# Two up products made while the last two tiles' gates are built, and two instead of three one-hot buffers in that gate building

## The chip, the cores and the metric

The kernel runs on one core of a Trainium2 chip. The metric is device time in microseconds (us), the median of the runs shown. The engines are named as in the profile: PE (TensorE matmuls, with PEld for its weight loads), DVE (VectorE), ACT (ScalarE), POOL (GpSimd, which issues the gathers) and SP (SyncE, which issues the other DMAs).

## The reference

The layer mixes 1024 tokens of width 1024 and then applies a PEER block: each token picks, for each of 8 heads, its 16 best of 16384 one-neuron experts and sums their outputs under a softmax gate.

```python
top, pos = lax.top_k(cand, PEER_TOPK)
idx = jnp.take_along_axis(cidx, pos, axis=-1)
gates = jax.nn.softmax(top, axis=-1)
u_sel = expert_u[idx]
act = gelu(einsum('thkd,td->thk', u_sel, xb))
v_sel = expert_v[idx]
return einsum('thk,thkd->td', gates * act, v_sel)
```

## The kernel before

The 8 tiles of 128 tokens are treated in two ways. Three tiles (0, 6, 7) are "sparse": the rows of u and v are gathered by POOL, and DVE forms the dot products (L547) and the weighted sums (L556). Five tiles (1 to 5; 640 tokens) are "dense": all 16384 experts are computed on PE in 128 blocks ("chunks") of 128 experts, and a dense gate matrix G, zero where an expert is not chosen, scales the activations.

The stages that matter here follow each other so:

- **Gate stage A** (`gates` with `who` "A", 48 blocks of 8 tokens for the first three dense tiles) is interleaved with the queries of the second half. **Gate stage B** (`who` "AT", 32 blocks for the last two dense tiles) comes after it, alone. A block makes two one-hot arrays and multiplies them on PE (L595), which gives the gates of 8 tokens. `o2` (L576, DVE, float32) is the first one-hot; `o1` (L582 or L588, DVE) the second; `og` is `o1` times the gate, made by ACT in 8 instructions (L585, an "A" block) or by DVE in one (L590, a "T" block). ACT moves the product from PSUM into `stg` (L597), and every fourth block SP stores `stg` to `G_dr` in HBM (L599). In the trace each 128x128 float32 matmul of L595 is recorded as two instructions. The buffer counts are three for `o2`, two for `og`, three for `o1`, four banks for the PSUM tile `pt`.
- **Dense stage**: `up(c)` loads the chunk's G (every fourth chunk, L639), u and v, splits u and v into a high and a low part (L183 on ACT, L184 on DVE), makes the up product on PE (24 matmuls for each half of the 640 tokens, tile `pu`), applies Gelu (L652, ACT), multiplies by G (L653, DVE) and splits the result (L656 on ACT, L657 on DVE). `down` multiplies the results of three chunks by v (tiles `pv` and `pa`), and DVE adds `pv` to the accumulators (L670).

In the kernel before, u of chunk 0 is loaded and split ahead of gate stage B (the name `u0`), and everything else of `up` lies behind it. When gate stage B ends, its SBUF pool and the PSUM pool are closed and the dense stage's pools take their place, so that tiles of the dense stage can lie where `stg` lay.

What order the instructions have on each engine is decided by the framework's planner: of the instructions that are ready by its own costs, it takes the one that was written first in the program. Each engine then runs its list in that order and stops at an instruction whose wait is not over. The sparse tiles' DVE work is written last and fills in; `pace` ties each piece from number 70 on to a chunk's first G product (`marks`). All loads and stores other than gathers are issued by SP, in order.

Of the kernel before, what the change touches and what calls it, by code (L numbers as in the profile page):

```python
# [45 lines left out]
GV = 3  # L46
AB = 2
GB = 3
RB = 4
VB = 7  # L50
DORD = [2, 0, 3, 1, 4]
# [20 lines left out]
def block_kernel(ctx: ExitStack, tc: tile.TileContext, x, attn_g, w_in, conv_w, sgu_wT, sgu_b, sgu_g,  # L72
# [119 lines left out]
    def mm3(o, lh, ll, rh, rl, first, last):  # L192
        pe.matmul(o, lh, rh, start=first, stop=False)  # L193
        pe.matmul(o, lh, rl, start=False, stop=False)  # L194
        pe.matmul(o, ll, rh, start=False, stop=last)  # L195
# [371 lines left out]
    def gates(pool, tiles, n0, n1, who):  # L567
        nblk = 0
        for n in range(n0, n1):
            stg = pool.tile([P, NCH // CB, TB, CB], F32, name="stg", bufs=2)  # L570
            for b in range(TB // OB):
                tt = n * TB + b * OB
                d, db = DT[tiles[tt // P]]
                tl = tt % P
                o2 = pool.tile([P, OB, P], F32, name="o2", bufs=3)
                v_.tensor_tensor(o2, iota_k.unsqueeze(1).to_broadcast([P, OB, P]),  # L576
                                 d[:, 0, tl:tl + OB].unsqueeze(2).to_broadcast([P, OB, P]), ALU.is_equal)
                nblk += 1
                og = pool.tile([P, OB, P], F32, name="og", bufs=OGB)
                if who[nblk % len(who)] == "A":  # L580
                    o1 = pool.tile([P, P, OB], BF16, name="o1", bufs=O1B)
                    v_.tensor_tensor(o1, iota_r, db[:, tl:tl + OB].unsqueeze(1).to_broadcast([P, P, OB]),  # L582
                                     ALU.is_equal)
                    for m in range(OB):
                        a_.activation(og[:, m, :], o1[:, :, m], AF.Copy, scale=d[:, 1, tl + m:tl + m + 1])  # L585
                else:
                    o1 = pool.tile([P, OB, P], BF16, name="o1", bufs=O1B)
                    v_.tensor_tensor(o1, iota_b.unsqueeze(1).to_broadcast([P, OB, P]),  # L588
                                     db[:, tl:tl + OB].unsqueeze(2).to_broadcast([P, OB, P]), ALU.is_equal)
                    v_.tensor_tensor(og, o1, d[:, 1, tl:tl + OB].unsqueeze(2).to_broadcast([P, OB, P]), ALU.mult)  # L590
                for q in range(OB // 4):
                    o = ps.tile([P, 4, P], F32, name="pt", bufs=4)
                    for i in range(4):
                        m = q * 4 + i
                        pe.matmul(o[:, i, :], o2[:, m, :], og[:, m, :], start=True, stop=True)  # L595
                    dst = stg[:, :, b * OB + q * 4:b * OB + q * 4 + 4, :].rearrange("p c t m -> p t c m")
                    a_.activation(dst, o.rearrange("p t (c m) -> p t c m", m=CB), AF.Copy)  # L597
                if b == TB // OB - 1:
                    nc.sync.dma_start(G_dr[:, :, n * TB:(n + 1) * TB, :], stg)  # L599
                yield  # L600
# [8 lines left out]
    def load(up_, src):  # L609
        raw = up_.tile([P, KC, P], F32, name="raw", bufs=RB)  # L610
        nc.sync.dma_start(raw, src)
        return split(up_, raw, [P, KC, P], "u", 2)

    def dense(pool, up_, pacc, pps, tiles, hD, u0):
        hTh, hTl = hD
        nt = len(tiles)
        HALF = TD // 2
        accs, full = {}, {}
# [16 lines left out]
        def up(c):  # L635
            if c % CB == 0:
                for hf in range(2):
                    Gt[hf] = pool.tile([P, HALF, CB], F32, name="G", bufs=GB)
                    nc.sync.dma_start(Gt[hf], G_dr[:, c // CB, hf * HALF:(hf + 1) * HALF, :])  # L639
            uh, ul = load(up_, peer_uT[c]) if c else u0  # L640
            raw = up_.tile([P, KC, P], F32, name="raw", bufs=RB)
            nc.sync.dma_start(raw, peer_v[c * P:(c + 1) * P, :].rearrange("e (k d) -> e k d", d=P))
            v = [split(pool, raw[:, 4 * dh:4 * dh + 4, :], [P, 4, P], "v", VB) for dh in range(2)]
# [1 line left out]
            wl = pool.tile([P, TD], F32R, name="wl", bufs=GV + 1)  # L645
            for hf in range(2):
                sl = slice(hf * HALF, (hf + 1) * HALF)
                o = pps.tile([P, HALF], F32, name="pu", bufs=2)
                for k in range(KC):
                    mm3(o, uh[:, k, :], ul[:, k, :], hTh[:, k, sl], hTl[:, k, sl], k == 0, k == KC - 1)  # L650
                a = pool.tile([P, HALF], F32, name="a", bufs=AB)
                a_.activation(a, o, AF.Gelu)  # L652
                gm = v_.tensor_tensor(a, a, Gt[hf][:, :, c % CB], ALU.mult)  # L653
                if hf == 0:
                    marks.append(gm)
                a_.activation(wh[:, sl], a, AF.Copy)  # L656
                v_.tensor_tensor(wl[:, sl], a, wh[:, sl].bitcast(F32), ALU.subtract)  # L657
# [79 lines left out]
    rx = ExitStack()  # L737
    hD = load_hD(sb(rx, "hdp", side="right"))
    up_ = sb(rx, "uvp", side="right")
    u0 = load(up_, peer_uT[0])  # L740
    with ExitStack() as c1:
        gp = sb(c1, "gpB")
        take(gates(gp, D_TILES, nA, NTB, OGPB))
    dkx.close()
    pre.close()
    with ExitStack() as c2:
        pool = sb(c2, "dl")
        pacc = c2.enter_context(tc.tile_pool(name="pacc", bufs=1, space=PSUM))
        pps = c2.enter_context(tc.tile_pool(name="pps", bufs=2, space=PSUM))
        dense(pool, up_, pacc, pps, D_TILES, hD, u0)  # L750
        sparse(spool, S_TILES)
    rx.close()

# [39 lines left out]
```

## Time and profile before

| What | Value |
|---|---|
| Median of 3 runs | 2833.63 us (2823.56 to 2846.36) |
| The profiled execution's own time | 2831.65 us |
| Its span | 2829.9 us, 40392 instructions |
| Busy share of the span: PE, DVE, ACT, POOL | 94%, 86%, 39%, 43% |
| Mean DMA rate | 251 GB/s |

The shares are means over stages with different limits. The stage before the gates ends near 628 us, gate stage A runs from about 628 to 902 us, gate stage B from about 905 to 998 us, and the dense stage fills the rest. PE's busy time is modelled from pipelined matmuls, so what a matmul costs is better read from the starts of a run of them.

### The profile page before, as it was taken

Reading aid. Unit: us, or ns where it says so; the run is one execution under the profiler, and the core shown is the slowest. Engines: PE = TensorE matmul, PEld = TensorE weight load, DVE = VectorE, ACT = ScalarE, POOL = GpSimd, SP = SyncE. Lnnn points to the kernel's source line nnn. Section 1 sums busy time; section 2 is a strip of 40 time slices with the busy share of each in tenths; the row PEclk is TensorE's granted clock in tenths of the full one; section 3 lists DMA queues with packets and bytes.
Section 4 is the critical chain, followed back from the end, with each engine's and each line's share of the span. In section 5 each row is a group of like instructions: output and inputs, shape, how many; then the busy total and the mean of one; then the engine's idle time right before and its main releaser. Section 6 shows DMA issues by size and latency. Waiting matters only on the chain.

```text
span 2829.9 us, 40392 instructions
## 1 busy us (share of the span) xinstructions
PE 2654.0 (94%) x14243; PEld 2325.6 (82%) x14243; DVE 2426.4 (86%) x4973; ACT 1102.9 (39%) x2125; POOL 1215.8 (43%) x1224
## 2 busy tenths in 40 slices
PE   8998889968885879999999999999999999999998
PEld 6876777756774768899888899899989889888987
DVE  3347978888989979999999999998998899898894
ACT  5324343249996932232333232323232222222223
POOL 0000013242002058777776666665555555455540
PEclk9999988888997999999999999999999999999999
DMA  3225225485447698988888897898888888888882
GB/s 123 82 81 191 81 69 172 137 304 150 141 125 264 197 348 313 332 297 318 324 301 323 314 325 292 310 333 314 306 323 316 303 318 305 296 325 282 305 320 75
DMA packets 270364, 709.96 MB, mean 251 GB/s; under 512 B 21576, under 2 KB 112720, under 8 KB 269904
## 3 DMA queue, kind: packets, MB, share of 16 engines
q0 software_dynamic: 110592, 402.70, 39.7%
q1 hardware_dynamic: 159568, 304.67, 31.2%
q8 instruction: 112, 1.84, 0.3%
q14 instruction: 92, 0.75, 0.1%
HBM read 650.14 MB, written 57.15 MB: 250 GB/s over the span
## 4 chain that ended last, share of the span: by engine, by line
PE 41%; DVE 16%; issue 7%; ACT 6%; DMA 5%; POOL 1%; SPq 0%; DVEq 0%; ACTq 0%; POOLq 0%
PE pu L193 6%; PE pu L194 6%; PE pu L195 6%; ACT og L585 4%; PE pv L193 4%; PE pv L195 4%; PE pv L194 4%; DVE gx L547 3%; DMA gx<-peer_u,si 3%; DVE acc L556 3%; PE pa L193 3%; PE pa L194 3%; PE pa L195 3%; PE pt L595 2%; DVE a L653 2%
## 5 line engine op out<-in xcount | busy, mean ns | idle before, releaser
L540 POOL DMA_INDIRECT gx<-peer_u,si x384 | 514.7, 1340 | 558.7 <-DVE dots L547 354.5
L540 POOL DMA_INDIRECT gx<-peer_v,si x384 | 538.3, 1402 | 350.8 <-DVE acc L556 239.1
L193 PE MATMUL pu<-hD,uh 128*128 128x320 f32 x2048 | 634.2, 310 | 17.3 <-ACT a L652 16.5
L195 PE MATMUL pu<-hD,ul 128*128 128x320 f32 x2048 | 633.5, 309 | 0.0
L194 PE MATMUL pu<-hD,uh 128*128 128x320 f32 x2048 | 633.3, 309 | 0.0
L556 DVE SCALAR_TENSOR_TENSOR acc<-gx,dots,acc 128x1024 f32<-128x1024 f32 x384 | 491.2, 1279 | 11.7 <-DMA gx<-peer_v,si 7.4
L547 DVE CUSTOM_DVE_ANT_0 gx<-gx,hn 128x1024 f32<-128x1024 f32 x384 | 460.1, 1217 | 16.3 <-DMA gx<-peer_u,si 13.5
L193 PEld LDWEIGHTS pu<-hD,uh 128*128 128x128 f32 x2048 | 384.9, 188 | 20.8 <-ACT a L652 18.3
L194 PEld LDWEIGHTS pu<-hD,uh 128*128 128x128 f32 x2048 | 385.2, 188 | 1.8
L195 PEld LDWEIGHTS pu<-hD,ul 128*128 128x128 f32 x2048 | 384.9, 188 | 0.0
L183 ACT ACTIVATE vh<-raw 128x512 fp32r<-128x512 f32 x256 | 160.9, 633 | 511.6 <-PE pv L195 487.8
L193 PE MATMUL pv<-vh,wh 128*128 128x512 f32 x768 | 302.2, 393 | 19.9 <-DVE ac L670 19.3
L656 ACT ACTIVATE wh<-a 128x320 fp32r<-128x320 f32 x256 | 120.9, 472 | 492.6 <-DVE a L653 479.4
L195 PE MATMUL pv<-vh,wl 128*128 128x512 f32 x768 | 301.1, 392 | 0.0
L194 PE MATMUL pv<-vl,wh 128*128 128x512 f32 x768 | 300.3, 391 | 0.0
L423 POOL TENSOR_TENSOR cidx<-i,i 128x8 f32<-128x8 f32 (+5 forms) x280 | 100.0, 386 | 361.3 <-DVE sel L450 163.1
L653 DVE TENSOR_TENSOR a<-a,G 128x320 f32<-128x320 f32 x256 | 186.6, 729 | 67.8 <-ACT a L652 67.8
L193 PE MATMUL pp<-Xh,wh 128*128 128x512 f32 x576 | 240.2, 418 | 3.1 <-ACT wh L183 3.1
L195 PE MATMUL pp<-Xh,wl 128*128 128x512 f32 x576 | 238.8, 415 | 3.3 <-DVE wl L184 3.3
L194 PE MATMUL pp<-Xl,wh 128*128 128x512 f32 x576 | 239.3, 416 | 0.0
L595 PE MATMUL pt<-og,o 128*128 128x128 f32 x1280 | 207.4, 306 | 30.1 <-ACT og L585 25.4
L585 ACT ACTIVATE og<-o,dT 128x128 f32<-128x128 bf16 x512 | 226.3, 518 | 5.8 <-DVE o L582 5.8
(188 smaller groups left out, 4670.9 us busy)
## 6 DMA issues: line engine op xcount, KB each, us to landing
raw<-peer_uT SPq DMA_DIRECT2D x128, 512.0 KB
raw<-peer_v SPq DMA_DIRECT2D x128, 512.0 KB
G_dr<-stg SPq DMA_DIRECT2D x20, 2048.0 KB
G<-G_dr SPq DMA_DIRECT2D x64, 640.0 KB
wraw<-w_in SPq DMA_DIRECT2D x40, 512.0 KB
wraw<-w_q SPq DMA_DIRECT2D x32, 512.0 KB
xt<-x SPq DMA_DIRECT2D x16, 512.0 KB
wraw<-w_out SPq DMA_DIRECT2D x16, 512.0 KB
```

The costliest lines, as they stand in the source:

```text
L183: a_.activation(hi, raw, AF.Copy)
L193: pe.matmul(o, lh, rh, start=first, stop=False)
L194: pe.matmul(o, lh, rl, start=False, stop=False)
L195: pe.matmul(o, ll, rh, start=False, stop=last)
L423: i = eng.tensor_tensor(dst[:, :, c:c + n], second[:, :, b0:b0 + n], first[:, :, a0:a1].to_broadcast([P, nt, n]), ALU.add)
L540: gp_.indirect_dma_start(out=gx, out_offset=None, in_=tab, in_offset=bass.IndirectOffsetOnAxis(ap=ii[:, s:s + 1], axis=0))
L547: pace(v_.tensor_tensor_reduce(gu, gu, hn, 1.0, 0.0, ALU.mult, ALU.add, dots[:, s:s + 1]), slot[0])
L556: pace(v_.scalar_tensor_tensor(acc, gv, dots[:, s:s + 1], acc, op0=ALU.mult, op1=ALU.add), slot[0])
L585: a_.activation(og[:, m, :], o1[:, :, m], AF.Copy, scale=d[:, 1, tl + m:tl + m + 1])
L595: pe.matmul(o[:, i, :], o2[:, m, :], og[:, m, :], start=True, stop=True)
L653: gm = v_.tensor_tensor(a, a, Gt[hf][:, :, c % CB], ALU.mult)
L656: a_.activation(wh[:, sl], a, AF.Copy)
```

## The change

A function `product` now makes an up product (24 matmuls and the Gelu for one half). For chunks 0 and 1 it is called from the gate stage B part: u of the chunk is loaded and split, both halves are multiplied into PSUM tiles of the tag `pp` (four banks that the queries used before and that the gate stage leaves alone), and the Gelu writes to two new SBUF tiles (`a0`, `a1`, 128x640 float32 each). Chunk 0 is written ahead of the first 16 blocks of stage B, chunk 1 ahead of the second 16. In the dense stage `up(0)` and `up(1)` then skip load, split, product and Gelu of u, and take the ready activations. The buffer count of `o2` is 2 in `gates`, which both gate stages call.

```diff
-                o2 = pool.tile([P, OB, P], F32, name="o2", bufs=3)
+                o2 = pool.tile([P, OB, P], F32, name="o2", bufs=2)
...
+    def product(pspool, tag, bufs, uh, ul, hD, sl, a):
+        o = pspool.tile([P, TD // 2], F32, name=tag, bufs=bufs)
+        for k in range(KC):
+            mm3(o, uh[:, k, :], ul[:, k, :], hD[0][:, k, sl], hD[1][:, k, sl], k == 0, k == KC - 1)
+        a_.activation(a, o, AF.Gelu)
...
-            uh, ul = load(up_, peer_uT[c]) if c else u0
+            pre_a = early.get(c)
+            if pre_a is None:
+                uh, ul = load(up_, peer_uT[c])
...
+                if pre_a is None:
+                    a = pool.tile([P, HALF], F32, name="a", bufs=AB)
+                    product(pps, "pu", 2, uh, ul, hD, sl, a)
+                else:
+                    a = pre_a[:, sl]
...
-    u0 = load(up_, peer_uT[0])
+    pf = sb(rx, "pf", side="right")
+    early = {}
     with ExitStack() as c1:
-        gp = sb(c1, "gpB")
-        take(gates(gp, D_TILES, nA, NTB, OGPB))
+        gg = gates(sb(c1, "gpB"), D_TILES, nA, NTB, OGPB)
+        nblk = (NTB - nA) * (TB // OB)
+        for c in range(PF):
+            early[c] = pf.tile([P, TD], F32, name=f"a{c}")
+            uh, ul = load(up_, peer_uT[c])
+            for hf in range(2):
+                sl = slice(hf * TD // 2, (hf + 1) * TD // 2)
+                product(ps, "pp", 4, uh, ul, hD, sl, early[c][:, sl])
+            take(gg, nblk // PF)
+        take(gg)
```

## Rows read from the trace of the kernel before

**Rows 1.** Page: busy time by engine, and the chain that ended last by engine.

```profile
PE 2654.0 (94%) x14243; PEld 2325.6 (82%) x14243; DVE 2426.4 (86%) x4973; ACT 1102.9 (39%) x2125; POOL 1215.8 (43%) x1224
...
PE 41%; DVE 16%; issue 7%; ACT 6%; DMA 5%; POOL 1%; SPq 0%; DVEq 0%; ACTq 0%; POOLq 0%
```

**Rows 2.** Busy time by stretch (columns in the first line).

```profile
core 0: us, PE busy (x) PEld busy (x) DVE busy (x) ACT busy (x) POOL busy (x), PEclk, DMA share, GB/s
628.00:902.00 274.00, 219.28 (x1221) 181.05 (x1219) 242.17 (x862) 240.29 (x550) 38.52 (x102) 0.90 0.52 155
905.00:998.00 93.00, 79.94 (x512) 66.82 (x512) 89.23 (x91) 87.69 (x194) 5.09 (x5) 0.95 0.74 237
998.00:1019.00 21.00, 7.30 (x48) 7.04 (x48) 8.26 (x11) 3.30 (x6) 9.96 (x8) 0.77 1.04 379
1019.00:1220.00 201.00, 191.85 (x1083) 174.51 (x1084) 195.44 (x330) 58.87 (x119) 154.51 (x126) 0.99 0.88 320
1220.00:1620.00 400.00, 395.90 (x2192) 357.35 (x2191) 386.86 (x684) 119.94 (x231) 271.78 (x252) 1.00 0.87 315
```

**Rows 3.** Waits in gate stage B: us in total, times, longest us.

```profile
PE pt L595 <- ACT og L585: 10.0, 31, 0.7
...
DVE o L576 <- PE pt L595: 3.1, 12, 0.6
```

**Rows 4.** Timeline of one pair of blocks in gate stage B: start, us, engine, line.

```profile
932.03 1.23 DVE L576 TENSOR_TENSOR o<-iota_k,dT 128x1024 f32<-128x1024 f32 x1 [0.23 <-PE pt L595]
...
934.74 2.18 ACT L585 ACTIVATE og<-o,dT 128x128 f32<-128x128 bf16 x5
...
937.50 1.23 DVE L576 TENSOR_TENSOR o<-iota_k,dT 128x1024 f32<-128x1024 f32 x1 [0.23 <-PE pt L595]
```

**Rows 5.** Timeline of a query step in gate stage A.

```profile
742.56 4.64 ACT L585 ACTIVATE og<-o,dT 128x128 f32<-128x128 bf16 x11
...
748.73 3.74 PE L595 MATMUL pt<-og,o 128*128 128x128 f32 x32
```

**Rows 6.** Waits in gate stage A.

```profile
DVE o L576 <- PE pt L595: 8.4, 8, 4.5
```

**Rows 7.** Timeline of the end of gate stage B and the first up product.

```profile
991.77 1.22 DVE L184 TENSOR_TENSOR ul<-raw,uh 128x1024 fp32r<-128x1024 f32 x1
...
993.01 0.34 SPq L642 DMA_DIRECT2D raw<-peer_v  x1
...
998.18 1.28 ACT L550 ACT_TABLE_LOAD   x1
...
998.22 0.41 PE L193 MATMUL pu<-hD,uh 128*128 128x320 f32 x1 [0.69 <-ACT stg L597]
...
1005.21 0.31 PE L195 MATMUL pu<-hD,ul 128*128 128x320 f32 x1
```

**Rows 8.** Chain that ended last, around the end of gate stage B: start, us, what.

```profile
998.19 20.68 DMA G_dr<-stg
...
1018.96 0.63 ACT vh L183
```

**Rows 9.** PE's waits, 1019 to 1220 us.

```profile
PE pu L193 <- ACT a L652: 16.1, 4, 14.4
PE pv L193 <- DVE ac L670: 6.6, 4, 1.9
```

**Rows 10.** DVE's waits, 1019 to 1220 us (the first began before 1019), then 1620 to 2800 us.

```profile
DVE vl L184 <- issue: 8.5, 1, 8.5
...
DVE a L653 <- ACT a L652: 53.9, 30, 2.2
```

**Rows 11.** Timeline of the start of the dense stage.

```profile
1023.20 3.92 DVE L556 SCALAR_TENSOR_TENSOR acc<-gx,dots,acc 128x1024 f32<-128x1024 f32 x3
...
1027.04 0.74 DVE L653 TENSOR_TENSOR a<-a,G 128x320 f32<-128x320 f32 x1
...
1029.47 0.44 ACT L652 ACTIVATE a<-pu 128x320 f32<-128x320 f32 x1 [1.19 <-DVE wl L657]
```

More of the change, by code (lines that the diff above doesn't have):

```diff
@@ L48 @@
 GB = 3
+PF = 2
 RB = 4
@@ L612, in load, with dense @@
         return split(up_, raw, [P, KC, P], "u", 2)
-    def dense(pool, up_, pacc, pps, tiles, hD, u0):
-        hTh, hTl = hD
+    def product(pspool, tag, bufs, uh, ul, hD, sl, a):
[3 more added lines that the diff above has]
+        a_.activation(a, o, AF.Gelu)
+    def dense(pool, up_, pacc, pps, tiles, hD, early):
         nt = len(tiles)
@@ L647, in up @@
                 sl = slice(hf * HALF, (hf + 1) * HALF)
[L648 to L652, printed above, removed]
+                if pre_a is None:
[3 more added lines that the diff above has]
+                    a = pre_a[:, sl]
                 gm = v_.tensor_tensor(a, a, Gt[hf][:, :, c % CB], ALU.mult)
@@ L749, in block_kernel @@
         pps = c2.enter_context(tc.tile_pool(name="pps", bufs=2, space=PSUM))
-        dense(pool, up_, pacc, pps, D_TILES, hD, u0)
+        dense(pool, up_, pacc, pps, D_TILES, hD, early)
         sparse(spool, S_TILES)
```

## The prediction

> **What bounds the kernel now.** I began with the page's busy shares and its chain of waits: PE is busy 94% of the span, but holds only 41% of the chain [rows 1]. So the limit changes by stage, and I cut the span at the two gate stages and the dense stage [rows 2].
>
> Gate stage B (905 to 998 us) is bound by ACT and DVE together: DVE is busy 89.2 of 93 us, ACT 87.7. PE shows 79.9, but that is modelled. In a stretch where the operands lie ready, 32 recorded matmuls of the gates take 3.74 us [rows 5], 0.117 us each; the 512 of stage B need 512 x 0.117 = 60 us. PE thus has 93 - 60 = 33 us free, in short waits for ACT's `og` (31 waits, 10.0 us in total beside the modelled time) [rows 3]. One pair of blocks (a T and an A) takes 937.50 - 932.03 = 5.47 us [rows 4]; 16 pairs are 87.5 us.
>
> What follows is not bound by PE. The last `stg` store is issued at 998.19 and lands 20.68 us later, at DMA share 1.04 [rows 2, 8]. ACT's split of v waits for it, because the v tiles lie where `stg` lay, and the chain runs through that wait. PE makes chunk 0's product in 7 us and then stands for 14.4 us: the Gelu that would free its PSUM tile is queued on ACT behind that split [rows 9]. From 1019 to 1220 us DVE is busy 195.4 of 201 us and almost never waits for PE; its largest wait in the answer, 8.5 us, lies before 1019 [rows 10]. PE waits for DVE there (6.6 us for L670). Only afterwards is PE the bound: 395.9 of 400 us from 1220 on [rows 2], and then DVE waits for PE (30 times, 53.9 us) [rows 10]. So the chain is: stage A, stage B, store landing, DVE for 200 us, PE to the end. What shortens PE ahead of 1220 us shortens the kernel only as far as DVE follows; what lengthens stage B moves everything.
>
> **The change, part by part.**
>
> *The products in stage B.* A product is 48 matmuls; the first starts at 998.22, the last at 1005.21 [rows 7], 0.149 us apart, so 7.1 us with the last one, 14.3 us for two. That fits PE's 33 us in sum. But PE runs its list in order, and all 48 become ready at once and were written ahead of the blocks that follow, so the planner will place them in one run. While PE is away, ACT can finish one A block's `og` (8 at 2.18/5 = 0.44 us, 3.5 us [rows 4]) and then has no free `og` buffer, since the two alternate between an A and a T block. It loses 7.1 - 3.5 = 3.6 us per product. In stage A the same pause of PE is covered: ACT keeps making `og` (11 in a row, 4.64 us) and PE then takes two blocks at a stroke [rows 5]; there both buffers are ACT's to fill. Ends: 0 (the matmuls fall singly into PE's waits) and 14.3 (nothing covered); I take 2 x 3.6 = 7.2, by the pair's own buffers. PSUM costs nothing: `pp` is idle.
>
> *What ACT gains in work.* Four Gelus of 0.44 us [rows 11] are 1.8 us, and the table load of 1.28 us that stood behind the gates, at the first Gelu of the sparse tiles [rows 7], now comes with the first early Gelu: 3.1 us. Both fall into the pause in which ACT waits for PE, so I add nothing if the pause is there, and 3.1 us if the products interleave. This is the floor of the lengthening. The Trainium skill, page "ScalarE: Activation LUTs", section What ACT_TABLE_LOAD costs, gives 1283 ns for the load, as the trace has, and about 1380 ns more for a drain; by it the floor would be 4.5 us and, uncovered, my sum 1.4 us more. The trace has no idle time that shows the drain.
>
> *What moves with the load of u.* The splits of u for chunk 0 and 1 were done inside stage B already; chunk 1's low part is DVE's last piece of it (1.22 us at 991.77) [rows 7], so DVE's sum there is unchanged. SP issues chunk 1's u ahead of the v loads; these loads wait for nothing of stage B, so no store is held behind them. The v load that stood at 993.01 waits for that last split [rows 7]; it now comes earlier and leaves the queues to the last store: 0.52 MB at 379 GB/s [rows 2] is 1.4 us. POOL's gathers are tied to the sparse work and are not moved.
>
> *Two `o2` buffers.* With three buffers DVE already waits 0.23 us for PE once in a pair [rows 4], 3.1 us over stage B [rows 3], 8.4 us over stage A [rows 6]. With two, block n's `o2` waits for the matmuls of block n-2, one block later than now. DVE is busy 96% of the stage [rows 2], so about 0.2 us of a pair are left; if the planner orders its pieces well it still fits, if not one piece of 1.22 us is exposed: 1.22 x 16 = 20 us. I take 2 us for stage B, near the waits shown. In stage A a late `o2` has ACT's whole `og` time as cover, against one exposed piece of 1.22 us in each of 16 query steps, 20 us; I take 1 us. A gain is excluded: fewer buffers take no wait away.
>
> *After the gates.* PE has 14.3 us less to do. Behind the last gate it makes chunk 2's product (7.1 us) and then has nothing until DVE multiplies the first activations by G, which was 1027.04 - 998.2 = 28.8 us after the last gate [rows 11]. Its pause grows from 14.4 to 28.8 - 7.1 = 21.7 us, so at most 14.3 - 7.3 = 7 us are left, and DVE, which sets the pace until 1220 us, has none of its 195 us removed. One thing can bring DVE forward: three sparse sums (3.92 us at 1023.20 [rows 11]) stand before the first G product and could run in DVE's pauses of stage B instead. Ends: 0 and 7 + 3.9 = 10.9 us gained; I take two thirds of the 3.9 us, 2.6, and the 1.4 us of DMA: 4.0.
>
> **Sum.** +7.2 + 2 + 1 - 4.0 = +6.2 us on the profiled execution's 2831.65 us: 2838 us. That execution lies 2 us below the median of the runs, far inside their spread of 23 us, so I leave it. By the skill's drain, if it is not covered, 2839.
>
> **Rivals.**
>
> *The products hide* (faster). The planner drops the 48 matmuls one by one into PE's waits. For it: 33 us free on PE, and chunk 1's u can be split early, which makes its product filler for the first 16 blocks. Against it: chunk 0's product is written ahead of all blocks. Then stage B grows by 3.1 us and up to 10.9 come back: 2831.65 - 7.8 = 2824 us.
>
> *Two one-hot buffers become the bound* (slower). In stage B the T block's `o2` and `og` both follow the previous T block's matmuls, and one DVE piece in between exposes 1.22 us in a pair; in stage A one piece in each query step. Price 20 + 20 = 40 us over the forecast's own other terms (6.2 - 3): 2831.65 + 43 = 2875 us. It decides from about 0.35 us a block (28 us over 80 blocks). For it: DVE waits for PE with three buffers already, and stage A and B have DVE 88 and 96% busy [rows 2]. Against it: `og` has had only two buffers all along. The Trainium skill, page "Trainium Kernel Development and Optimization", section Best Practices, says that consistent bubbles can mean that buffer memory ran out; the steady 0.23 us in each pair agrees.
>
> *It does not do what it says.* Chunk 1's low split, which stood last on DVE in stage B, stays late, and its product is made behind the gates after all. Then one pause of 3.6 us and little gain: about 2834 us.
>
> **How the numbers follow.** What a measurement of this kernel can tell from no change is 1%, 28 us. Forecast 0.58 (its own range 2828 to 2852); hidden products 0.20; no early second product 0.12; one-hot bound 0.10. The range that holds the first three with their bounds, and the nearer part of the last, is 2821 to 2858. Slower by over 1% (above 2862) takes 0.07 from the one-hot case and next to nothing else; faster by over 1% (below 2805) needs more than the 14.3 us of PE work that is moved, so 0.02, for a different order of the whole plan; the rest, 0.91, is within 1%.
>
> **What would show it.** Right: stage B about 10 us longer, two gaps in ACT's `og` rows at two runs of 48 `pp` matmuls; one longer pause of PE after the gates, near 22 us; the stretch from store landing to 1220 us as full on DVE as now. Wrong: a stage B that grows by 3 us or less; a first G product earlier than 25 us after the last gate; or waits of DVE's `o2` for PE over 20 us in sum.

## The result and the profile after

The changed kernel takes 2855.38 us (median of 12 runs, 2844.22 to 2864.40), the kernel before, on the same chip, 2824.16 us (12 runs): a ratio of 1.0091, 95% interval 1.0070 to 1.0111, which is 26 us more. A ratio here is worked out from the runs of both kernels without the few that were much slower, and is not the quotient of the medians that stand beside it (1.0111, or 31 us, for these two). The forecast was 2838 us, 6 us more, within a range up to 2858. The time lies in the range and the sign is that of the sum, but the sum was four times too small.

The profiled execution of the changed kernel took 2855.61 us (span 2853.8, against 2829.9). I cut both spans at the same four places: the first `o2` of gate stage A, its last store of `stg`, the last store of stage B, the end.

| Stretch | before, us | after, us | difference | forecast |
|---|---|---|---|---|
| start to the first `o2` | 628.1 | 627.3 | -0.8 | 0 |
| stage A, first `o2` to last store | 254.3 | 260.9 | +6.6 | +1 |
| stage B, to its last store | 115.9 | 132.5 | +16.6 | +9.2 |
| last store to the end | 1831.7 | 1833.1 | +1.4 | -4.0 |

So nearly all of the loss lies in the two gate stages, and the gain that should have come behind them did not come.

The page of the changed kernel: busy time by engine, and the chain that ended last by engine (against [rows 1]).

```profile
PE 2659.0 (93%) x14243; PEld 2333.4 (82%) x14243; DVE 2426.9 (85%) x4973; ACT 1103.1 (39%) x2125; POOL 1214.7 (43%) x1224
...
PE 39%; DVE 18%; issue 7%; ACT 6%; DMA 5%; POOL 2%; DVEq 0%; POOLq 0%; SPq 0%; ACTq 0%
```

Every engine has the work it had; the span grew by waits. Busy time by stretch in the changed kernel: stage A, stage B, two parts of stage B, then the counterpart of the line of [rows 2] that begins at 1019 us.

```profile
core 0: us, PE busy (x) PEld busy (x) DVE busy (x) ACT busy (x) POOL busy (x), PEclk, DMA share, GB/s
628.00:908.70 280.70, 213.95 (x1221) 179.96 (x1219) 245.00 (x865) 240.31 (x552) 49.75 (x104) 0.89 0.52 154
908.70:1020.50 111.80, 98.94 (x608) 86.67 (x608) 94.67 (x97) 93.79 (x201) 9.43 (x7) 0.91 0.69 224
931.20:966.65 35.45, 33.73 (x236) 29.77 (x235) 30.77 (x30) 32.87 (x75) 1.67 (x1) 1.00 0.75 223
966.65:1020.70 54.05, 46.33 (x251) 38.34 (x249) 43.56 (x47) 45.20 (x97) 2.87 (x2) 0.87 0.58 168
1044.00:1245.00 201.00, 190.13 (x1029) 170.11 (x1029) 190.53 (x328) 58.55 (x118) 136.28 (x121) 0.98 0.84 301
```

In stage B before, DVE was busy 96% of the time [rows 2]; in the last 54 us of it now 43.56 of 54.05, 81%, and no other engine has taken its place as the full one. The granted clock is 1.00 while the second product fills PE (931 to 967) and 0.87 after it, a mean over both levels, 2.4 GHz (1.00) and 1.2 GHz (0.50). These rows show that DVE lost time and that PE ran slower; the waits say for what. Waits of the changed kernel in stage B (us in total, times, longest), against [rows 3]:

```profile
DVE o L577 <- PE pt L596: 15.2, 14, 1.6
ACT stg L598 <- PE pt L596: 10.0, 15, 1.2
PE pt L596 <- ACT og L586: 7.7, 15, 0.7
```

and the same in stage A, against [rows 6]:

```profile
DVE o L577 <- PE pt L596: 10.9, 10, 3.4
PE pt L596 <- DVE o L577: 4.9, 5, 1.9
```

DVE's `o2` waits for PE 15.2 + 10.9 = 26.1 us in the two stages; it was 3.1 + 8.4 = 11.5. The second line of stage A is new: PE waits for an `o2` that was late. The timeline of a late pair of blocks (start, us, engine, line), against [rows 4]:

```profile
1003.42 4.75 PE L596 MATMUL pt<-og,o 128*128 128x128 f32 x30 [0.56 <-ACT og L586]
...
1006.43 1.23 DVE L577 TENSOR_TENSOR o<-iota_k,dT 128x1024 f32<-128x1024 f32 x1 [1.59 <-PE pt L596]
...
1013.14 1.23 DVE L577 TENSOR_TENSOR o<-iota_k,dT 128x1024 f32<-128x1024 f32 x1 [1.48 <-PE pt L596]
```

A pair takes 1013.14 - 1006.43 = 6.71 us; it was 5.47. The wait in it went from 0.23 to 1.5 us: nearly the whole difference is this one wait.

The two products do not behave alike. The stores of `stg` in stage B (one for every four blocks) came every 10.9 us before, after a first one 38.5 us behind the last store of stage A and a second 11.9 later. Now the intervals are 43.0, 10.9, 12.3, 12.2, 13.3, 13.5, 13.6 and 13.6 us: +4.6, -0.9, +1.4, +1.3, and then +2.4 to +2.7 for each of the last four, which lie behind both products. Timeline of the first product in the changed kernel, its first and last matmul and the table load for the first early Gelu:

```profile
920.04 0.41 PE L194 MATMUL pp<-hD,uh 128*128 128x320 f32 x1 [0.98 <-ACT uh L184]
...
924.00 1.28 ACT L619 ACT_TABLE_LOAD   x1
...
927.71 0.31 PE L196 MATMUL pp<-hD,ul 128*128 128x320 f32 x1
```

It is one run of 48 matmuls (with six of the gates' in it), as forecast. The second was not: its matmuls fell between the gates' from 931 to 960 us, one to seven at a time.

Behind the gates, from the chain that ended last (start, us, what), against [rows 8]:

```profile
1020.69 21.62 DMA G_dr<-stg
...
1042.39 2.71 ACT vh L184 x5
```

DVE's first product with G in the changed kernel, against [rows 11]:

```profile
1047.93 2.10 DVE L661 TENSOR_TENSOR a<-a,G 128x320 f32<-128x320 f32 x3 [0.75 <-DMA G<-G_dr]
```

and PE's waits from 1020 to 1245 us, against [rows 9]:

```profile
PE pu L194 <- ACT a L619: 21.9, 4, 17.5
PE pv L194 <- DVE ac L678: 3.6, 5, 1.5
```

The landing of the last store still holds ACT's splits of v, and the Gelu behind them still holds PE.

### The profile page after: what moved, and what is told of

It is laid out like the page before. It is cut to its first block, busy times and chain, and to the rows that moved or that the text cites. A ratio compares the mean times of both kernels' runs of the same rounds, so it can differ in the third digit from the quotient of the medians.

```text
span 2853.8 us, 40377 instructions
## 1 busy us (share of the span) xinstructions
PE 2659.0 (93%) x14243; PEld 2333.4 (82%) x14243; DVE 2426.9 (85%) x4973; ACT 1103.1 (39%) x2125; POOL 1214.7 (43%) x1224
## 4 chain that ended last, share of the span: by engine, by line
PE 39%; DVE 18%; issue 7%; ACT 6%; DMA 5%; POOL 2%; DVEq 0%; POOLq 0%; SPq 0%; ACTq 0%
PE pu L194 6%; PE pu L195 6%; PE pu L196 6%; ACT og L586 4%; DVE gx L548 4%; PE pv L194 4%; PE pv L196 4%; PE pv L195 4%; PE pt L596 3%; DMA gx<-peer_u,si 3%; PE pa L195 2%; PE pa L194 2%; PE pa L196 2%; DVE acc L557 2%; DVE a L661 2%
## 5 line engine op out<-in xcount | busy, mean ns | idle before, releaser
L541 POOL DMA_INDIRECT gx<-peer_v,si x384 | 524.7, 1367 | 469.3 <-DVE acc L557 263.9
L194 PE MATMUL pu<-hD,uh 128*128 128x320 f32 x2016 | 625.4, 310 | 24.0 <-ACT a L619 23.3
L196 PE MATMUL pu<-hD,ul 128*128 128x320 f32 x2016 | 624.5, 310 | 0.0
L195 PE MATMUL pu<-hD,uh 128*128 128x320 f32 x2016 | 624.2, 310 | 0.0
L557 DVE SCALAR_TENSOR_TENSOR acc<-gx,dots,acc 128x1024 f32<-128x1024 f32 x384 | 491.7, 1280 | 13.4 <-DMA gx<-peer_v,si 9.0
L194 PEld LDWEIGHTS pu<-hD,uh 128*128 128x128 f32 x2016 | 379.7, 188 | 27.9 <-ACT a L619 25.3
L195 PEld LDWEIGHTS pu<-hD,uh 128*128 128x128 f32 x2016 | 379.9, 188 | 1.8
L194 PE MATMUL pv<-vh,wh 128*128 128x512 f32 x768 | 303.2, 395 | 22.9 <-DVE ac L678 22.4
L424 POOL TENSOR_TENSOR cidx<-i,i 128x8 f32<-128x8 f32 (+5 forms) x280 | 105.2, 405 | 346.7 <-DVE sel L451 157.6
L596 PEld LDWEIGHTS pt<-og,o 128*128 128x128 f32 x1280 | 180.3, 211 | 62.1 <-ACT og L586 42.4
```

Source lines behind the costliest of these rows:

```text
L424: i = eng.tensor_tensor(dst[:, :, c:c + n], second[:, :, b0:b0 + n], first[:, :, a0:a1].to_broadcast([P, nt, n]), ALU.add)
L541: gp_.indirect_dma_start(out=gx, out_offset=None, in_=tab, in_offset=bass.IndirectOffsetOnAxis(ap=ii[:, s:s + 1], axis=0))
L557: pace(v_.scalar_tensor_tensor(acc, gv, dots[:, s:s + 1], acc, op0=ALU.mult, op1=ALU.add), slot[0])
```

## The experiments

Each is compared with the kernel before, run on the same chip as it; the chips of different rows can differ, and two ratios whose intervals overlap are not clearly apart. The first table gives the times, the second where the time lies, from one profiled execution each, cut as above. The start of stage A moves by up to 13 us from profile to profile for reasons ahead of the change, so a stage is read by its own length.

| Kernel | median, us (runs) | before, us | ratio [95%] |
|---|---|---|---|
| changed kernel | 2855.38 (12) | 2824.16 | 1.0091 [1.0070, 1.0111] |
| e1 early products, three `o2` | 2831.46 (12) | 2827.15 | 1.0026 [1.0005, 1.0048] |
| e2 two `o2` in stage B alone | 2840.95 (7) | 2827.15 | 1.0062 [1.0039, 1.0086] |
| e3 two `o2` in stage A alone | 2834.68 (8) | 2827.15 | 1.0040 [1.0016, 1.0064] |
| e4 early products as fill-in | 2821.06 (12) | 2827.15 | 0.9980 [0.9963, 0.9997] |
| f1 before, no wait for the store | 2833.49 (12) | 2829.37 | 1.0020 [1.0004, 1.0037] |
| f2 e1, no wait for the store | 2843.03 (8) | 2829.37 | 1.0049 [1.0031, 1.0067] |
| f3 before, sparse work later | 2842.60 (7) | 2829.37 | 1.0046 [1.0023, 1.0068] |
| f4 e1, sparse work later | 2840.10 (12) | 2829.37 | 1.0047 [1.0030, 1.0065] |
| g1 e1, products woven in | 2835.47 (12) | 2830.70 | 1.0029 [1.0011, 1.0047] |
| g2 e2 with PE kept busy | 2836.49 (10) | 2830.70 | 1.0016 [0.9996, 1.0036] |
| g3 changed kernel, PE kept busy | 2846.72 (10) | 2829.24 | 1.0053 [1.0034, 1.0072] |
| g4 before, PE kept busy | 2831.06 (12) | 2829.24 | 1.0005 [0.9983, 1.0026] |

"Chunk 10" and "chunk 30" are the starts of these chunks' first G product after the last store.

| Kernel | stage A | stage B | store to end | chunk 10 | chunk 30 |
|---|---|---|---|---|---|
| before | 254.3 | 115.9 | 1831.7 | 162.5 | 431.9 |
| changed | 260.9 | 132.5 | 1833.1 | 154.4 | 433.6 |
| e1 | 253.4 | 122.8 | 1823.6 | 153.2 | 432.1 |
| e2 | 251.7 | 132.2 | 1830.1 | 164.4 | 435.9 |
| e3 | 261.0 | 115.6 | 1828.1 | 165.6 | 434.6 |
| e4 | 253.5 | 114.5 | 1830.5 | 156.0 | 432.8 |
| f1 | 254.4 | 118.1 | 1827.2 | 164.3 | 434.2 |
| f2 | 254.2 | 123.7 | 1832.3 | 157.7 | 439.0 |
| f3 | 251.8 | 115.6 | 1843.0 | 157.6 | 430.3 |
| f4 | 254.5 | 122.9 | 1838.7 | 150.9 | 423.1 |
| g1 | 253.5 | 120.8 | 1835.8 | 155.6 | 437.4 |
| g2 | 252.7 | 121.2 | 1830.1 | 162.1 | 432.6 |
| g3 | 265.0 | 132.8 | 1818.2 | 144.5 | 424.4 |
| g4 | 253.0 | 118.2 | 1830.7 | 162.1 | 431.5 |

### The two parts of the change, one at a time (e1, e2, e3)

e1 is the changed kernel with the third `o2` given back; so that it fits, `a0` and one half of `a1` lie in tiles of another pool.

```diff
-                o2 = pool.tile([P, OB, P], F32, name="o2", bufs=2)
+                o2 = pool.tile([P, OB, P], F32, name="o2", bufs=3)
...
-            early[c] = pf.tile([P, TD], F32, name=f"a{c}")
+            if c == 0:
+                a = ks.tile([P, TD], F32, name="sel")
+                early[c] = [a[:, :TD // 2], a[:, TD // 2:]]
+            else:
+                early[c] = [ks.tile([P, TD // 2], F32, name="eq"), pf.tile([P, TD // 2], F32, name="a1")]
...
```

> The changed kernel with three one-hot buffers again; to make room, the early activations lie in buffers of the choose step that stand idle then. Theory (the third buffer's loss is the larger part): the last gate store, 22.5 us late in the changed kernel, is only 6 to 10 us late, stage B's later stores come every 10.9 us as before (13.5 in the changed kernel), stage A ends as before, DVE's o2 waits for PE fall from 15.2 us in stage B to about 3; the whole is 6 to 10 us over the kernel before, 0.2 to 0.35%. Rival (the early products on PE are the larger part): the last store stays 15 us or more late and the whole 0.6 to 0.9% over before.

e2 and e3 are the kernel before with two `o2` in one of the stages:

```diff
-                o2 = pool.tile([P, OB, P], F32, name="o2", bufs=3)
+                o2 = pool.tile([P, OB, P], F32, name="o2", bufs=3 if who == "A" else 2)
...
+                o2 = pool.tile([P, OB, P], F32, name="o2", bufs=2 if who == "A" else 3)
```

> The kernel before with two one-hot buffers in stage B alone. Theory: each pair of blocks waits about 1.3 us more, a store 2.6 us more, 8 stores 18 to 21 us; the last store at about 1017 us and the whole 16 to 21 us (0.6 to 0.75%) over before. Rival (the 13.5 us beat of the changed kernel's later stores was set off by the early products, and two buffers alone are enough): stores every 10.9 to 11.5 us, the whole within 5 us of before.

> The kernel before with two one-hot buffers in stage A alone. Theory: stage B starts 3 to 5 us later, as in the changed kernel (3.8 us), and the whole is 3 to 5 us (0.1 to 0.2%) over before. Rival (a late o2 is covered by ACT's og time, and the 3.8 us came from another order): within 1 us of before.

With three `o2`, the early products lengthen stage B by 122.8 - 115.9 = 6.9 us (intervals of the stores 43.3, 10.9, 12.1, 12.4, 11.2, and then 10.9 as before). With two `o2` and no early product, stage B grows by 16.3 us (intervals 38.5, 12.7, 13.1, 13.4, and then 13.5 to 13.7) and stage A, in e3, by 6.7. Stage A took 251.7 to 254.5 us in the eleven kernels that have three `o2` there, and 260.9, 261.0 and 265.0 in the three that have two. By the ratios the early products cost 0.26% and the buffer, as the difference between the changed kernel and e1, 0.65%, 18 us. e3 as a whole is 0.40% slower, 11 us (interval 5 to 18), more than the 3 to 5 expected; its one profile has the 6.7 us in stage A and is as a whole 0.4 us longer than that of the kernel before, so where the 11 us lie is not shown.

A stretch of stage B behind the second product in e1, and its `o2` wait over the stage:

```profile
962.20:1006.30 44.10, 38.42 (x252) 31.40 (x250) 42.41 (x45) 43.28 (x98) 3.52 (x2) 1.00 0.71 206
```

```profile
DVE o L577 <- PE pt L596: 5.5, 16, 1.0
```

The middle of stage B in e2, its waits and its timeline:

```profile
952.40:993.10 40.70, 35.41 (x193) 29.31 (x193) 31.38 (x31) 33.46 (x72) 0.00 (x0) 0.88 0.53 155
```

```profile
DVE o L576 <- PE pt L595: 19.2, 14, 1.7
ACT stg L597 <- PE pt L595: 10.2, 18, 1.1
```

```profile
965.31 1.23 DVE L576 TENSOR_TENSOR o<-iota_k,dT 128x1024 f32<-128x1024 f32 x1 [1.50 <-PE pt L595]
...
972.17 1.23 DVE L576 TENSOR_TENSOR o<-iota_k,dT 128x1024 f32<-128x1024 f32 x1 [1.63 <-PE pt L595]
```

The three intervals of four blocks in this stretch hold the same instructions as three of the kernel before, where they took 32.70 us at a granted clock of 1.00 (here 40.70 at 0.88):

```profile
954.50:987.20 32.70, 29.15 (x194) 24.05 (x193) 31.34 (x31) 32.13 (x73) 0.00 (x0) 1.00 0.66 193
```

DVE has the same 31 instructions and 31.3 to 31.4 us of work in both; in e2 it stands for the rest. In e3 the `o2` wait of stage A is that of the changed kernel:

```profile
DVE o L576 <- PE pt L595: 10.8, 10, 3.4
PE pt L595 <- DVE o L576: 4.9, 5, 1.9
```

So the buffer is the larger part, in both stages. In the changed kernel stage B pays for it only in its last half: up to the fourth store, 78.5 us behind stage A's last one, it is level with e1 (78.8), and the last four intervals bring the remaining 54.0 - 44.0 = 10.0 us. Two things differ between the halves. In the first the products keep PE busy, at clock 1.00. And DVE's order differs: in the kernel before, the `o1` of an "A" block stands ahead of the `o2` that waits, as the row ahead of the first `o2` of [rows 4] shows:

```profile
931.12 0.68 DVE L582 TENSOR_TENSOR o<-iota_r,dTb 128x1024 bf16<-128x1024 bf16 x1
```

In the changed kernel the two orders alternate from 945 to 964 us, and from there on the waiting `o2` stands first in every pair, as in e2 from 923 us to the end.

### Is it the buffer, or PE's clock? (g2, g4, g3)

Two readings were left: two buffers make a longer loop whatever PE does; or they make PE wait, the granted clock falls, the matmuls for which DVE waits take longer, and the wait grows. Work that nobody needs, put on PE so that it waits less, should cost time by the first, and save time by the second, as long as the planner leaves the order of the other engines alone. Behind the matmuls of each block of stage B stand three more, on constants, with an unused result:

```diff
-                        pe.matmul(o[:, i, :], o2[:, m, :], og[:, m, :], start=True, stop=True)
+                        last = pe.matmul(o[:, i, :], o2[:, m, :], og[:, m, :], start=True, stop=True)
...
+                if who != "A":
+                    dm = ps.tile([P, 512], F32, name="pp", bufs=4)
+                    for i in range(3):
+                        after(pe.matmul(dm, iota_b, iota_r[:, 0:64, :].rearrange("p a b -> p (a b)"), start=True, stop=True), last)
```

g2 is e2 with it, g4 the kernel before, g3 the changed kernel.

> Two one-hot buffers in stage B alone, with three bfloat16 matmuls of 512 columns on constants added behind each of its 32 blocks (about 0.65 us of PE work a block, results unused). Theory (half of the new wait is PE's clock, which falls to 0.88 of full speed in stage B when PE waits more): the granted clock there is 0.97 or more and the stores come every 12.0 to 12.6 us, against 13.6 without the added matmuls and 10.9 with three buffers; stage B gets shorter although PE has more to do. Rival (the loop over the buffers alone makes the beat): 13.6 us or more.

> The kernel before (three o2) with the same added matmuls in gate stage B. Its clock is at 1.00 there already and DVE hardly waits for PE, so both theories expect the store period at 10.9 to 11.2 us and the whole within 3 us of the kernel before. If it gains more than 3 us, the gain of the added matmuls has nothing to do with two buffers; if it loses more, the added matmuls have a price of their own that must be taken off in the other runs.

> The changed kernel with three more matmuls (128x512, on constants, result unused) behind each block of gate stage B. Theory 'the fallen clock stretches what DVE waits for': the granted clock after the second product stays at 1.00 (it was 0.87), the last four stores come every 12 us or less in place of 13.5, and from the last store of stage A to the last of stage B it takes 126 to 131 us in place of 132.5, the median is 3 to 8 us lower than the changed kernel's ratio of 1.0091 gives (1.006 to 1.008 here). Rival 'only the number of buffers counts': the last four stores stay at 13.5 us or grow, ratio 1.009 or more.

Stage B in g2, from its third store to its last, its waits and its timeline:

```profile
932.50:991.40 58.90, 57.09 (x380) 45.90 (x379) 53.00 (x54) 54.18 (x120) 2.00 (x2) 1.00 0.64 188
```

```profile
DVE o L576 <- PE pt L595: 7.5, 11, 1.1
ACT stg L597 <- PE pt L595: 4.1, 5, 0.9
```

```profile
954.49 0.69 DVE L582 TENSOR_TENSOR o<-iota_r,dTb 128x1024 bf16<-128x1024 bf16 x1
...
955.66 0.81 PE L601 MATMUL pp<-iota_r,iota_b 128*128 128x512 bf16 x3
955.86 1.23 DVE L576 TENSOR_TENSOR o<-iota_k,dT 128x1024 f32<-128x1024 f32 x1 [0.68 <-PE pt L595]
...
961.35 1.23 DVE L576 TENSOR_TENSOR o<-iota_k,dT 128x1024 f32<-128x1024 f32 x1 [0.70 <-PE pt L595]
...
962.49 0.68 DVE L582 TENSOR_TENSOR o<-iota_r,dTb 128x1024 bf16<-128x1024 bf16 x1
```

With 96 matmuls more, the stage is 11 us shorter: 121.2 against 132.2 us, the whole 1.0016 against 1.0062. The clock is 1.00 again, the wait in a pair 0.68 in place of 1.5 us, its total 7.5 in place of 19.2. The kernel before gains nothing from the same matmuls; they lengthen its stage B from 115.9 to 118.2 us, with a store every 11.4 us, a little more than expected. So with the added matmuls two `o2` cost 121.2 - 118.2 = 3.0 us in stage B, and 16.3 without them.

That difference is not the clock's alone. The added matmuls also changed the planner's order: in g2 the pairs alternate, `o1` ahead of the waiting `o2` in one (954.49, 955.86) and behind it in the next (961.35, 962.49), where e2 has it behind in every pair. And e2's own trace shows what its order costs at full clock. Here are three of its iterations, each from the start of one row of seven `og` on ACT to the start of the next, and ACT's and DVE's part in the last of them:

```profile
928.05:934.45 6.40, 5.25 (x34) 4.17 (x32) 5.24 (x6) 5.58 (x13) 0.00 (x0) 1.00 0.98 282
961.41:968.60 7.19, 6.74 (x34) 5.65 (x32) 5.70 (x7) 5.58 (x14) 0.00 (x0) 0.76 0.20 59
968.60:975.00 6.40, 5.09 (x32) 4.17 (x32) 4.77 (x5) 5.57 (x13) 0.00 (x0) 1.00 0.89 261
```

```profile
968.60 3.00 ACT L585 ACTIVATE og<-o,dT 128x128 f32<-128x128 bf16 x7
...
973.32 0.69 DVE L582 TENSOR_TENSOR o<-iota_r,dTb 128x1024 bf16<-128x1024 bf16 x1
...
975.00 3.01 ACT L585 ACTIVATE og<-o,dT 128x128 f32<-128x128 bf16 x7
```

The first lies ahead of the first such fall of the clock (from 905 to 934 us it is 1.00 throughout) and takes 6.40 us already, against 5.47 with three buffers. Later iterations at 1.00 and at 0.76 alternate, 6.40 and 7.19 us, and the `o2` wait is no shorter at full clock: 1.63 us at 972.17, in an iteration at 1.00, and 1.50 us at 965.31, in one at 0.76. At full clock the loop is a series: ACT's seven `og` feed PE's matmuls of the A block; the `o2` of the next A block waits for the last of them (972.17); that block's `o1` stands behind the `o2` (973.32), and ACT's next `og` behind the `o1` and one copy into `stg` (975.00). As an estimate from these rows, four blocks take 2 x 6.40 = 12.8 us at full clock in this order, 6.40 + 7.19 = 13.6 as measured, and 10.9 before: of the 2.7 us that two buffers cost, 1.9 are the loop and 0.8 the clock. Of the 1.6 us that g2 then wins back (13.6 to 12.0) the clock thus explains about half; the rest goes with the other order, which no run shows by itself. A kernel with PE kept busy and e2's order was not run.

The rows of g3 and then g4, over three and four of their last intervals:

```profile
993.00:1027.90 34.90, 33.68 (x224) 27.49 (x228) 31.18 (x29) 32.44 (x73) 5.86 (x3) 1.00 0.69 201
```

```profile
953.60:999.10 45.50, 45.24 (x299) 37.01 (x303) 43.25 (x45) 43.91 (x96) 3.67 (x2) 1.00 0.69 202
```

In g3 the clock is 1.00 to the end too, the last three intervals are 12.0, 11.0 and 12.0 us in place of 13.5 to 13.6, and the ratio falls from 1.0091 to 1.0053, 11 us, more than the 3 to 8 expected (the intervals just touch). The expected length of stage B was missed (132.8 us): one interval of 18.0 us holds dot products, sparse sums and a split of u (979.4 to 985.4 us on DVE) which in the changed kernel stood later, some behind the gates; they come back as a first G product 18.4 us after the last store in place of 27.2, and an end 14.9 us closer to it. So in the profiles g3 wins nothing in stage B and all of its gain behind it; since its order differs too, it does not show the size of the clock's part.

### Where the gain behind the gates went (f1 to f4)

In e1 and in the changed kernel chunk 10 is 8 to 9 us ahead of the kernel before, of 14.3 us that were moved; at chunk 30 the lead is gone. Two things could take it: the wait for the last store, or DVE. f1 (the kernel before) and f2 (e1) place `stg` behind other tiles and load G after v, so that the splits of v wait for no store:

```diff
-            stg = pool.tile([P, NCH // CB, TB, CB], F32, name="stg", bufs=2)
+            stg = None
...
+                if stg is None:
+                    stg = pool.tile([P, NCH // CB, TB, CB], F32, name="stg", bufs=2)
...
+        v_.memset(pool.tile([P, HALF], F32, name="a", bufs=AB)[:, 0:1], 0.0)
...
-            if c % CB == 0:
-                for hf in range(2):
-                    Gt[hf] = pool.tile([P, HALF, CB], F32, name="G", bufs=GB)
...
             v = [split(pool, raw[:, 4 * dh:4 * dh + 4, :], [P, 4, P], "v", VB) for dh in range(2)]
+            if c % CB == 0:
+                for hf in range(2):
+                    Gt[hf] = pool.tile([P, HALF, CB], F32, name="G", bufs=GB)
...
```

> The kernel before, with the tiles of the gate stage and of the dense stage in another order in SBUF, so that neither the v tiles nor the activations lie where stg lay; only G and the scaled activations still wait for the last store. Theory (behind the gates the store's landing and then DVE set the pace, not PE): PE's pause of 14.4 us shrinks below 8 us, but the first product with G stays 26 to 30 us behind the last gate, DVE stays full until about 1220 us, and the end gains at most 5 us, 0 to 0.2%. Rival (PE's pause is what costs): 9 to 14 us gained, 0.3 to 0.5%.

> The first experiment's kernel (early products, three one-hot buffers) with the same other order in SBUF. Theory: as above, 0 to 5 us better than that kernel was, so +2 to +8 us against before. Rival (with nothing waiting for the store, PE is the limit and the moved products pay): 10 us or more better, 3 us or more under before.

The pause stayed, above the 8 us expected, and changed its name. PE's longest wait behind the gates in f1, and in f2:

```profile
PE pa L193 <- ACT wh L659: 10.4, 1, 10.4
```

```profile
PE pv L194 <- ACT wh L667: 17.4, 1, 17.4
```

`wh` needs G, and G can be loaded only when the last store has landed. f1 gained nothing (1.0020) and f2 lost 0.23% against e1, which I had not expected (their intervals overlap): in f2 the wait is longer than in f1, and at chunk 30 it is 7 us behind e1. The wait for the store is real, but what lies where is not its cause.

f3 (the kernel before) and f4 (e1) give DVE less to do at the start of the dense stage: the sparse pieces are tied to chunks up to four later.

```diff
-            k = int((n - NFREE) * NCH * PACE / (len(S_TILES) * 2 * P - NFREE))
+            k = int(4 + (n - NFREE) * (NCH - 4) * PACE / (len(S_TILES) * 2 * P - NFREE))
```

> The kernel before with the paced sparse pieces spread over chunks 4 to 127 instead of 0 to 127, which takes about 22 of them (27 us) from DVE's first 60 us of the dense stage and spreads them over the rest. Theory (DVE holds the first 200 us behind the gates): PE's waits for L670 there (6.6 us) nearly go, the first G product comes up to 4 us earlier, the end gains 3 to 9 us (0.1 to 0.3%). Rival (DVE is no limit there): within 2 us, or slower, since DVE has more to do later.

> The first experiment's kernel with the sparse pieces later in the same way. Theory (DVE is why the products moved out of the dense stage did not pay): with DVE relieved they pay 4 to 7 us, so this kernel is 0 to +4 us against the one with sparse pieces later alone, where it was +7 without. Rival (the moved products cannot pay, whatever DVE does, since PE pauses for G): again +6 to +9 us over that one.

Now the lead of the early products stays: f4 is 6.7 us ahead of f3 at chunk 10 and 7.2 at chunk 30, and as a whole the two are level (1.0047 and 1.0046), so the lead about pays for the longer stage B, as was expected if DVE is the limit. Both kernels are slower than before, though, by 0.46 and 0.47%, where f3 was expected to gain 3 to 9 us. The work put off comes back where DVE has no room for it; PE's waits for DVE in f3 from 1430 to 2600 us are 22.9 us in 15, where the kernel before has 12.7 us in 10 over the same stretch behind the last store:

```profile
PE pv L193 <- DVE ac L670: 22.9, 15, 5.0
```

Busy time from 160 to 435 us after the last store (about chunks 10 to 30), of the kernel before, of e1 and of f4:

```profile
1158.20:1433.20 275.00, 271.93 (x1537) 247.54 (x1536) 268.91 (x472) 82.79 (x163) 200.31 (x187) 1.00 0.85 309
```

```profile
1166.30:1441.30 275.00, 264.60 (x1467) 237.19 (x1468) 268.84 (x462) 79.41 (x159) 205.84 (x184) 1.00 0.87 317
```

```profile
1156.90:1431.90 275.00, 270.94 (x1507) 244.63 (x1506) 269.00 (x477) 81.64 (x160) 198.28 (x181) 1.00 0.86 312
```

DVE is full in each, 268.8 to 269.0 of 275 us. In e1 PE makes 70 matmuls fewer than before in this stretch and is busy 7 us less: that is the lead going back. It is gone by chunk 20 already (297.8 us behind the last store, 296.0 before).

### Other places for the products (g1, e4)

g1 is e1 with each product cut into 16 pieces of three matmuls, one written ahead of each block:

```diff
-                product(ps, "pp", 4, uh, ul, hD, sl, early[c][hf])
-            take(gg, nblk // PF)
+                o = ps.tile([P, TD // 2], F32, name="pp", bufs=4)
+                for k in range(KC):
+                    mm3(o, uh[:, k, :], ul[:, k, :], hD[0][:, k, sl], hD[1][:, k, sl], k == 0, k == KC - 1)
+                    take(gg, 1)
+                a_.activation(early[c][hf], o, AF.Gelu)
```

e4 is e1 with both products written behind all blocks, so that they only fill in:

```diff
-        nblk = (NTB - nA) * (TB // OB)
+        take(gg)
         for c in range(PF):
...
-            take(gg, nblk // PF)
-        take(gg)
```

> The first experiment's kernel (early products, three one-hot buffers), with each product written in 16 pieces of 3 matmuls, one ahead of each gate block, so that the planner weaves them into PE's waits. Theory: no run of 48 matmuls, so stage B is 1 to 4 us longer than before instead of 7; the lead behind the gates at chunk 10 (8 to 9 us in the early kernels) is there but is gone by chunk 30, where DVE is the limit; the whole within 4 us of before. Rival (the lead survives if stage B does not pay for it): 5 to 9 us under before, 0.2 to 0.3%.

> As the first of these runs (three one-hot buffers), but both products are written behind the last gate block, so that the planner takes them only where it sees PE idle. Theory: no run of 48 matmuls, stage B 0 to 4 us longer than before, so the last store 4 to 7 us earlier than in the first run; and the end follows the last store to within 5 us, since the stretch behind the gates is held by the store's landing and by DVE: the whole 0 to +4 us against before. Rival (PE is the limit behind the gates too): the end gains the 14.3 us of moved products, 8 to 12 us under before, 0.3 to 0.4%.

Woven in, stage B grows by 4.9 in place of 6.9 us, and the whole is 0.29% slower, 8 us (3 to 13), where at most 4 us were expected; the lead of 6.9 us at chunk 10 is gone by chunk 30 again. As fill-in, 77 of the products' 96 matmuls start behind the last store, from 995.9 to 1007.1 us, in the pause that PE has there anyway; stage B grows by nothing (114.5 us), and PE's longest wait there falls from 14.4 to 11.7 us, the last number of this row:

```profile
PE pu L194 <- ACT a L619: 13.2, 3, 11.7
```

This is the only version that beats the kernel before, by 0.20% (0.03 to 0.37), 6 us. Neither guess had that: 0 to 4 us slower was expected, and the rival said 8 to 12 us faster.

## Why the prediction was right and wrong

**Two `o2` buffers: the step that failed.** I took 2 us for stage B and 1 for stage A. Measured: 10 us in stage B of the changed kernel (16.3 alone, e2) and 6.6 in stage A (6.7 alone, e3). I chose the lower end "if the planner orders its pieces well it still fits", from 0.2 us of room in a pair. Without a product beside it the planner did not order them so: it put the `o2` that waits ahead of the "A" block's `o1`, and DVE and ACT then work in series, 6.40 us a pair in place of 5.47 at full clock. The upper end, one piece of 1.22 us exposed in a pair, is met in size by the wait, 1.5 - 0.23 = 1.27 us, but the way there is another: about 0.9 us of a pair is this loop, and about 0.4 is PE's clock, which I had left where it was when I called PE's 33 free us a reserve. At full clock the last eight pairs would still have cost 8 x 0.93 = 7.4 us by e2's iterations (an estimate), not 2. In stage A the granted clock is 0.89 against 0.90 [rows 2], so its 6.6 us are not the clock's; which order or wait makes them was not taken apart. The rival of the one-hot bound had this price for stage B, with a chance of 0.10; its 20 us in stage A were three times too much. By its own mark (0.35 us a block) it decided: in the last eight pairs a block cost (6.75 - 5.47)/2 = 0.64 us more (54.0 us for eight pairs). The sign that I had named for "wrong", over 20 us of `o2` waiting for PE, came up with 26.1. The Trainium skill, page "Trainium Kernel Development and Optimization", section Best Practices, says that consistent bubbles can mean that SBUF or PSUM ran out; the trace agrees: the bubble was in [rows 4] before a buffer was taken away, 0.23 us with three and 1.5 with two.

**The products in stage B: the sum right, half of it by luck.** 2 x 3.6 = 7.2 us forecast, 6.9 measured (e1), as 4.85 - 0.93 = 3.9 around the first and 1.2 + 1.5 + 0.3 = 3.0 around the second. The first is one run, as described; that it costs its 3.9 us through `og` was not tested. The second fell in small groups between the gates, as the "hide" rival had it, so the sign that I had named, two runs of 48, did not come; and yet it cost 3 us. PE's product matmuls stand between the gates' there, and DVE's `o2` waits for PE 5.5 us over e1's stage B in place of 3.1, which is most of the 3 us.

**ACT's table load: right.** It moved to 924.00, 1.28 us, between the first product's matmuls, and the first Gelu follows at 925.29. No time for a drain behind it shows, so the smaller sum held.

**After the gates: the gain did not show.** I took 4.0 us of gain; the profile shows a loss of 1.4, and e1, which has the same products, is by its ratio 7 us slower (1 to 14) where its stage B alone costs 6.9, so the rest is about nothing. The few us are not settled: from the last store to the end, the one profile of e1 is 8.1 us shorter than before, most of it behind chunk 60, while e3 and f1, without early products, are 3.6 and 4.5 shorter. The reason that I gave for taking little, that DVE sets the pace until 1220 us and none of its work is removed, holds from the first G product on and was not followed far enough: the lead at chunk 10 is gone by chunk 20, and with less work on DVE (f4 against f3) it stays. The first G product came 1.6 us earlier after the last store (27.25 against 28.85), not 4. Of the two terms the sparse sums came in: from the store's landing to that product it is 1047.93 - 1042.31 = 5.6 us, where it was 1027.04 - 1018.87 = 8.2, which is the 2.6 that I took. The 1.4 us of DMA did not: the store took 0.9 us longer to land (21.62 against 20.68), not 1.4 less. PE's pause ended not with the first G product, as I had it (21.7 us), but with the Gelu that frees its PSUM tile, 17.5 us.

**The rivals.** *The products hide* needed them to fall into PE's waits; one of the two did, at 3 us, and g1, where both do, still pays 4.9 us in stage B and ends slower than before; hiding was not to be had by this. e4 is 8.3 us shorter than e1 in stage B, and 13 us by the ratios; what makes the rest is not shown. *It does not do what it says*: the change did what it says; both products lay inside stage B.

**Range and chances.** The time of 2855 us is inside the range only because the range took in the nearer part of the one-hot case; the forecast's own range ended at 2852. Luck helped as well: the kernel before ran at 2824.16 us here, 7.5 us below the execution to which the sum was added, and the 31 us between the medians on top of 2831.65 would have been 2863. The loss of 0.91% is just under the bound of 1%; I had given a chance of 0.91 to staying within it.

The size thus comes out so, in the profiles: 6.9 us for the products (taken from e1), 10 and 6.6 for the buffer, 1.4 behind the gates, less 0.8 at the start, 24 us in all.

## What to carry to other kernels

Before a buffer is taken from a loop, look in the timeline for a wait that it already causes: here a steady 0.23 us in each round left no room, and the bound "one piece of work exposed per round" was near the price, not an upper end out of reach. Write down which engine then waits for which, in the order in which the planner places the pieces: two engines that worked side by side with three buffers worked in series with two. When PE waits more, look at the clock column of the stretch, not at the span's mean, but compare single rounds at either level before the loss is put down to the clock: here it was under a third of it. And a test that adds work can change the order of everything else; compare the order too. Work moved ahead of a barrier pays only if the engine that sets the pace behind it gets room too; follow the lead along the chunks to see who takes it.

## What was not expected of the hardware

Ninety-six useless matmuls made a stage of the kernel 11 us shorter (132.2 to 121.2): the granted clock stayed at 1.00 in place of 0.88, and the planner's order changed. The waits of PE ahead of the first fall of the clock are short, 0.40 and 0.75 us by turns in e2; in the kernel before, whose clock stays at 1.00, they are 0.4 and 0.2. The Trainium skill, page "TensorE: Matmul & The Clock Gate", section "A second HAM failure mode: psum-queue depth-cycling", tells of a kernel whose PE pauses briefly but often between groups of matmuls and swings between the two clock levels; the trace of e2 agrees in kind, with 0.88 over the stretch. The price of it was smaller than it looked: with three buffers four blocks take 10.9 us at 1.00, with two 13.6, and two of e2's iterations at 1.00 would be 12.8 (an estimate), so that the lower level costs 0.8 of the 2.7 us. With two buffers, a busy PE and the other order they take 11 to 12.
